# A decoder trunk on one core: row sums ordered behind weight splits, two homes for branch weights, an early weight's split ordered behind the last output weight's

## The chip, the core and the metric

The kernel runs on one core of a Trainium2 chip. A core has five engines that run side by side, each through its own stream of instructions in order: TensorE (PE; matrix products, with PEld its weight loads), VectorE (DVE), ScalarE (ACT), GpSimd (POOL) and SyncE (SP, which here only issues transfers). The metric is the device time of one execution in microseconds (us), as the median of several runs. The profile is of one further execution.

## The reference

One layer of a decoder trunk on x of 512 tokens by 1024 channels, in float32: a conditioned norm, one input projection, two attention branches, two gates, an output projection with residual, then a second conditioned norm and a gated MLP with a short convolution.

```python
mod = cs @ w_ada[l] + b_ada[l]
shift1, scale1, gate1, shift2, scale2, gate2 = [m[:, None, :] for m in jnp.split(mod, 6, axis=-1)]
h = _rmsnorm(x, norm1_g[l]) * (1.0 + scale1) + shift1
proj = h @ w_in[l]
qa, ka, va, qd, kd, vd, ga, gd = jnp.split(proj, points, axis=-1)
...
merged = (jax.nn.sigmoid(ga) * (out_a @ w_branch_swa[l])
          + jax.nn.sigmoid(gd) * (out_d @ w_branch_diff[l]))
x = x + gate1 * (merged @ w_out[l])
h2 = _rmsnorm(x, norm2_g[l]) * (1.0 + scale2) + shift2
x = x + gate2 * _conv_ffn(h2, w_up[l], conv_w[l], conv_b[l], w_down[l])
return _rmsnorm(x, final_g)
```

## The kernel before

Every float32 product is made of three products of split operands: a value is split into a high part (a cast on ScalarE, L102) and a low part (a subtraction on VectorE, L103), and high by high, high by low and low by high are summed (`mm3`, L105). So each weight that arrives from memory passes ScalarE, then VectorE, then TensorE. Such a pass is called a split here. `split_pair` (L95) makes it into two rotating buffers, tags "whi" and "wlo" with three places each; `split` (L101) makes it into a tile that is given.

Raw weights arrive in tiles of 512 KB with the tag "raw", which has four places for all of them (`raw_tile`, L90). A place is free again when its last reader is done, so a weight that waits for its split keeps the next load back.

The stages, in order: the input projection's first part; the sliding-window attention; the differential attention with the "a" gates; from tick 182 the "d" gates and the merge (eight gate units `wgd`, `pgd` of eight steps, and eight branch units `wbd`, `pB` of four steps, interleaved, L860 to L897); the output projection (`wo`, `oc`); the norm; the MLP's up products (`up`, a scheme that multiplies sums and differences of blocks; its first operands are p1, p2 and m5); the down products (`dc`).

Until the merge is done, TensorE's order is written out by hand through `fill` (L459): each call is one tick, which runs one step of the current unit and loads up to two units ahead (`prefetch`, L454). At the ticks in `ADA_AT` (L30) one further row of the modulation weight is loaded and summed on VectorE: `ada_rows` (L706), 32 rows in all, 17 of them at ticks up to 148 and 15 from tick 180 to 250. These sums give gate1, shift2, scale2 and gate2, which are needed when the output weights are scaled (`g1b`) and after the merge (`g2row`, spread over partitions by TensorE transposes and copied by ScalarE).

The other engines' streams are laid down when the program is built, by a planner. It takes instructions in source order, or by priority where one is given, and its own estimate of when each is ready; on the chip each engine then follows its stream. `tc.high_priority` lets instructions go ahead; `tc.issue_after(ins)` puts those of the same engine as `ins` behind `ins` in the stream, at build, without a wait on the chip. In `ada_rows` the sums have high priority and come behind `behind_dve`, in this stage a VectorE instruction of the attention that has long passed.

The branch weight `wbd` holds two units' weights, so four are made, j = 0, 2, 4 and 6. All four are split into one tile, `gpart(3)` (tag "gT3", one place). Later that tile serves `st` (L1051), whose first half `s_t` is filled by two transfers: a plain load by SP, and one that adds a second block to it, issued by POOL (L1002, L1004). Its split is m5, into a tile of the tag "m5w" (L1059), which nothing else uses before.

The output weights are scaled and split by `load_rows` (L930, `wo`, `wo_h`, `wo_l`), eight of them, two or three ahead of TensorE since "whi" and "wlo" have three places. The early weights p1 and p2 (L1055) come after them in the source, in tiles of their own (`early`). p2's low part is ordered behind the last output weight's low part, `wo_low`.

Of the kernel before, what the change touches and what calls it, by code (L numbers as in the profile page):

```python
# [8 lines left out]
F32 = mybir.dt.float32  # L9
F32R = mybir.dt.float32r  # L10
# [4 lines left out]
P = 128  # L15
D = 1024
S = 512
KT = D // P
# [8 lines left out]
WB = 3  # L27
HP = 100000
ST = 6
ADA_AT = set(range(20, 150, 8)) | set(range(180, 300, 5))  # L30
G1_AT = 12
STAT_LAG = 10
# [9 lines left out]
def kernel(  # L42
# [19 lines left out]
    nc = tc.nc  # L62
    xd, wout, wup, wdown = x[0], w_out[0], w_up[0], w_down[0]
    wba, wbd, od = w_branch_swa[0], w_branch_diff[0], out[0]

    def pool(name, bufs=1, space=None, stack=ctx):
        kw = {} if space is None else {"space": space}
        return stack.enter_context(tc.tile_pool(name=name, bufs=bufs, reuse_waits="tile", **kw))
# [12 lines left out]
    def sbank(name, shape=(P, S)):  # L81
        return bank("s", 3, list(shape), name)
# [7 lines left out]
    def raw_tile(shape, name):  # L90
        return wp.tile(shape, F32, tag="raw", bufs=4, name=name)

    lows = [None]

    def split_pair(raw, shape, name):  # L95
        hi = wp.tile(shape, F32R, tag="whi", bufs=WB, name=name + "_h")
        lo = wp.tile(shape, F32R, tag="wlo", bufs=WB, name=name + "_l")
        lows[0] = split(hi, lo, raw)
        return hi, lo

    def split(hi, lo, src):  # L101
        nc.scalar.copy(hi, src)  # L102
        return nc.vector.tensor_sub(lo, src, hi.bitcast(F32))  # L103

    def mm3(o, lh, ll, rh, rl, start, stop):  # L105
        nc.tensor.matmul(o, lh, rh, start=start, stop=False)  # L106
# [337 lines left out]
    def load_tile(n, name):  # L444
        r = raw_tile([P, KT, P], name)
        nc.sync.dma_start(r, w_tiles[n])
        return split_pair(r, [P, KT, P], name)
# [4 lines left out]
    current, tick, behind_dve = [], [0], [None]  # L452
# [6 lines left out]
    def fill(n):  # L459
        for _ in range(n):  # L460
# [19 lines left out]
            tick[0] += 1  # L480
            if tick[0] in ADA_AT:
                next(ada, None)
# [4 lines left out]
    def steps(o, wts, rhs, nk, k0=0, cl=slice(0, P)):  # L487
        wh, wl = wts
        for k in range(nk):
            mm3(o, wh[:, k, cl], wl[:, k, cl], rhs[0][k0 + k], rhs[1][k0 + k], k == 0, k == nk - 1)  # L490
            if k < nk - 1:
                yield
# [7 lines left out]
    def swa_scores(i, n0):  # L500
        if n0 == 0:
# [4 lines left out]
            c.sb = [ap.tile([P, 2, P], F32, tag="st0", bufs=2, name=f"st{i}_0")]  # L506
            c.sb += [ap.tile([P, 2, 256], F32, tag="st", bufs=ST, name=f"st{i}_{n}") for n in range(1, NT)]
            c.pT = []
# [100 lines left out]
    def diff_scores(*ss):  # L609
# [17 lines left out]
        for s, sps, w in ops:  # L627
# [3 lines left out]
            for m in range(2):  # L631
                st = ap.tile([P, w], F32, tag="st", bufs=ST, name=f"sd{h}_{n}_{m}")
                with tc.high_priority(offset=HP):
# [72 lines left out]
    def ada_rows():  # L706
        for idx in range(32):
            r = raw_tile([P, D], f"ra{idx}")
            nc.sync.dma_start(r, w_ada_t[2 * D + idx * P : 2 * D + (idx + 1) * P, :])
            with tc.high_priority(offset=HP // 2), tc.issue_after(behind_dve[0].ins):  # L710
                nc.vector.tensor_tensor_reduce(r, r, csb, 1.0, 0.0, ALU.mult, ALU.add, late_mod[:, idx : idx + 1])  # L711
            yield

# [3 lines left out]
    def add_gate_a(j):  # L717
        def gate(wts):
            o = fbank(f"pga{j}")
            yield from steps(o, wts, hT, KT)  # L720
            with tc.high_priority(offset=HP):
                nc.scalar.activation(ta[:, j], o, AF.Tanh, scale=0.5)

        def load():
            if j % 2 == 0:
                r = raw_tile([P, 4, 2 * P], f"wba{j}")
                for a in range(2):
                    nc.sync.dma_start(
                        r[64 * a : 64 * a + 64],
                        wba[256 * a : 256 * a + 256, j * P : (j + 2) * P].rearrange("(i p) n -> p i n", p=64),  # L730
                    )
                pair_w["a"] = split_pair(r, [P, 4, 2 * P], f"wba{j}")
            return pair_w["a"]

        def branch(wts):
            o = fbank(f"pA{j}")
            rhs = [[outa[b][:, k] for k in range(4)] for b in range(2)]
            yield from steps(o, wts, rhs, 4, cl=slice(j % 2 * P, j % 2 * P + P))
            nc.vector.scalar_tensor_tensor(ta[:, j], ta[:, j], 1.0, o, ALU.add, ALU.mult)

        units.append((lambda: load_tile(TILE_GA + j, f"wga{j}"), gate))
        units.append((load, branch))

    pairs, firsts, scored, probs, aTs = {}, {}, {}, {}, {}
    ada = ada_rows()
    add_q(2)
    add_q(3)
# [80 lines left out]
    bp = pool("mlp")  # L828

    def gpart(i, shape, name, dt=F32):  # L830
        if i < 2:
            return big.tile(shape, dt, tag=("vvh", "vvl")[i], name=name)
        return bp.tile(shape, dt, tag=f"gT{i}", name=name)
# [9 lines left out]
    g1b = gpart(4, [P, D], "g1b")  # L843
# [25 lines left out]
    def add_merge(j):  # L869
        def load():  # L870
            if j % 2 == 0:
                r = raw_tile([P, 4, 2 * P], f"wbd{j}")
                nc.sync.dma_start(r, wbd[:, j * P : (j + 2) * P].rearrange("(i p) n -> p i n", p=P))
                wb = gpart(3, [P, 2, 4, 2 * P], f"wbd{j}", F32R)
                wh, wl = wb[:, 0], wb[:, 1]
                split(wh, wl, r)
                pair_w["d"] = wh, wl
            return pair_w["d"]

        def branch(wts):  # L880
            o = sbank(f"pB{j}")
            rhs = [[vv[b][:, k] for k in range(4)] for b in range(2)]
            yield from steps(o, wts, rhs, 4, cl=slice(j % 2 * P, j % 2 * P + P))
            td = tds[j]
            nc.vector.scalar_tensor_tensor(td, td, 1.0, o, ALU.add, ALU.mult)
            nc.vector.tensor_add(td, td, ta[:, j])
            split(mgh[j], mgl[j], td)

        units.append((load, branch))
# [32 lines left out]
    def eight(name):  # L922
        return [
            [tbank(name + "0"), tbank(name + "1")],
            [fbank(name + "2"), fbank(name + "3")],
            [sbank(name + "4"), sbank(name + "5")],
            [sbank(name + "6"), vbank(name + "7")],
        ]

    def load_rows(src, k, name, gate):  # L930
        r = raw_tile([P, D], name)
        nc.sync.dma_start(r, src[k * P : (k + 1) * P, :])
        nc.vector.tensor_mul(r, r, gate)
        pair = split_pair(r, [P, D], name)
        return pair

    def tok_proj(acc, lh, ll, wts, nk, done, half_done=None):
        def step(k, t, hfs=(0, 1)):
# [24 lines left out]
    bl = big.tile([P, 3, 4, 256], F32R, tag="hlA", name="bl")  # L963
    braw = {}
    oacc = eight("oc")
    wo = [load_rows(wout, k, f"wo{k}", g1b) for k in range(KT)]

    def add_and_stat(acc, dst, x, wpool, name):
        ss = []
# [29 lines left out]
    W, R = {}, {}  # L999

    def load_raw(dst, blocks):
        nc.sync.dma_start(dst, upblock(*blocks[0]))  # L1002
        for blk in blocks[1:]:
            nc.gpsimd.dma_start(dst, upblock(*blk), accum_op=ALU.add)  # L1004
        return dst
# [16 lines left out]
    SRC = dict(p1="a11", m5="s1", m6="s1", p2="a12", m7="s3", p3="s1", p4="a22")  # L1022

    def sum_w(J, name):
        src = R[J, SRC[name]]
        nc.vector.tensor_add(src, src, R[J, "a11" if name == "m6" else "a12"])  # L1026

    def cast_w(J, name):
        W[J, name] = [
            wp.tile([P, 4, 256], F32R, tag=g, bufs=WB, name=f"{name}_{J}_{g}") for g in ("whi", "wlo")  # L1030
        ]
        nc.scalar.copy(W[J, name][0], R[J, SRC[name]])  # L1032

    def low_w(J, name):
        hi, lo = W[J, name]
        nc.vector.tensor_sub(lo, R[J, SRC[name]], hi.bitcast(F32))  # L1036

    def prep(J, name, dst=None):
        if dst is not None:
            W[J, name] = dst  # L1040
            return split(dst[0], dst[1], R[J, SRC[name]])
        if name in ("m6", "p3"):
            sum_w(J, name)
        cast_w(J, name)
        low_w(J, name)
# [5 lines left out]
    st = gpart(3, [P, 2, 4, 256], "s1_t1")  # L1051
    t1n = st[:, 1]
    R[0, "s1"] = load_raw(st[:, 0], [(0, 1, 0), (0, 1, 1)])
    wo_low = lows[0]
    for i, name in enumerate(("p1", "p2")):  # L1055
        with tc.issue_after(wo_low.ins) if i else ExitStack():
            early_low = prep(0, name, (early_w[i][:, 0], early_w[i][:, 1]))
        W[1, name] = early_w[2 + i][:, 0], early_w[2 + i][:, 1]
    m5w = bp.tile([P, 2, 4, 256], F32R, tag="m5w", name="m5w")  # L1059
    prep(0, "m5", (m5w[:, 0], m5w[:, 1]))  # L1060
    with tc.issue_after(early_low.ins):
        sum_w(0, "m6")
# [371 lines left out]
    for x in range(2):  # L1434
        prep(*ahead.pop(0))
# [336 lines left out]
```

## Time and profile before

| | before |
|---|---|
| median of 3 runs | 688.33 us (688.19 to 689.62) |
| the profiled execution | 686.36 us |
| its span, first to last instruction | 684.6 us |
| mean granted TensorE clock | 0.998 |
| busy: TensorE, its weight loads | 673.5 (98%), 589.6 (86%) |
| busy: VectorE, ScalarE, GpSimd | 556.8 (81%), 383.5 (56%), 65.9 (10%) |
| bytes moved | 119.68 MB, mean 175 GB/s |
| chain that ended last, by engine | PE 78%, DMA 9%, DVE 8%, issue 3%, ACT 1% |

A row of the timeline gives the start in us, the duration in us, the engine, the line of the kernel, the operation, output and inputs, how many were merged, and in brackets the engine's idle time before it and what ended it. A row with a count (x32) and three durations gives the shortest, median and longest in ns and the first and last start. In the list of waits the numbers are us in total, times and the longest. A busy TensorE is not one at its peak, since the ends of matmuls are modelled.

### The profile page before, as it was taken

Reading aid. Unit: us, or ns where it says so; the run is one execution under the profiler, and the core shown is the slowest. Engines: PE = TensorE matmul, PEld = TensorE weight load, DVE = VectorE, ACT = ScalarE, POOL = GpSimd, SP = SyncE. Lnnn points to the kernel's source line nnn. Section 1 sums busy time; section 2 is a strip of 40 time slices with the busy share of each in tenths; the row PEclk is TensorE's granted clock in tenths of the full one; section 3 lists DMA queues with packets and bytes.
Section 4 is the critical chain, followed back from the end, with each engine's and each line's share of the span. In section 5 each row is a group of like instructions: output and inputs, shape, how many; then the busy total and the mean of one; then the engine's idle time right before and its main releaser. Section 6 shows DMA issues by size and latency. Waiting matters only on the chain.

```text
span 684.6 us, 10929 instructions
## 1 busy us (share of the span) xinstructions
PE 673.5 (98%) x4117; PEld 589.6 (86%) x4117; DVE 556.8 (81%) x1036; ACT 383.5 (56%) x678; POOL 65.9 (10%) x74
## 2 busy tenths in 40 slices
PE   8999999999999999999999999999999999999995
PEld 7887777778788888788799999999999998888884
DVE  5996867778775677773689998888888999979997
ACT  6676756454554332441588565666555666656665
POOL 2000000000100000000020110111110003540300
PEclk9999999999999999999999999999999999999999
DMA  9952224454363667347672989787866658996903
GB/s 355 417 214 79 94 85 149 145 170 150 97 183 94 200 236 245 119 161 226 197 124 83 215 226 209 177 200 186 204 170 184 152 171 198 199 204 187 165 1 124
DMA packets 71077, 119.68 MB, mean 175 GB/s; under 512 B 3952, under 2 KB 47728, under 8 KB 71024
## 3 DMA queue, kind: packets, MB, share of 16 engines
q1 hardware_dynamic: 52960, 95.04, 41.8%
q0 software_dynamic: 17776, 23.60, 21.1%
q8 instruction: 32, 0.52, 0.3%
q10 hardware_dynamic: 288, 0.34, 0.2%
q14 instruction: 21, 0.17, 0.1%
HBM read 116.87 MB, written 2.10 MB: 174 GB/s over the span
## 4 chain that ended last, share of the span: by engine, by line
PE 78%; DMA 9%; DVE 8%; issue 3%; ACT 1%; DVEq 0%; POOLq 0%; ACTq 0%
PE up L1098 32%; PE dc L1701 11%; DMA ra<-in_w_ada_t_dram 4%; PE av L345 3%; DMA s_t<-in_w_up_dram 2%; PE pga L106 2%; PE aqa L342 2%; PE pga L107 2%; PE pga L108 2%; PE sd L113 1%; PE pk L106 1%; PE pq L106 1%; DVE ra L711 1%; PE pk L108 1%; PE pq L108 1%
## 5 line engine op out<-in xcount | busy, mean ns | idle before, releaser
L1098 PE MATMUL up<-t,m_whi 128*128 128x256 f32 x512 | 93.1, 283 | 0.0
L1098 PEld LDWEIGHTS up<-t,m_whi 128*128 128x128 f32 x512 | 79.9, 192 | 0.0
L1098 PE MATMUL up<-t,m_wlo 128*128 128x256 f32 x256 | 72.4, 283 | 0.0
L1098 PE MATMUL up<-bh,p_whi 128*128 128x256 f32 x232 | 65.7, 283 | 0.0
L1098 PE MATMUL up<-bl,p_whi 128*128 128x256 f32 x232 | 65.7, 283 | 0.0
L1098 PE MATMUL up<-bh,p_wlo 128*128 128x256 f32 x232 | 65.7, 283 | 0.0
L711 DVE CUSTOM_DVE_ANT_0 ra<-ra,csb 128x1024 f32<-128x1024 f32 x32 | 39.0, 1220 | 16.5 <-DMA ra<-in_w_ada_t_dram 16.5
L1098 PEld LDWEIGHTS up<-t,m_wlo 128*128 128x128 f32 x256 | 49.2, 192 | 0.0
L1098 PEld LDWEIGHTS up<-bh,p_whi 128*128 128x128 f32 x232 | 44.5, 192 | 0.0
L1098 PEld LDWEIGHTS up<-bl,p_whi 128*128 128x128 f32 x232 | 44.5, 192 | 0.0
L1098 PEld LDWEIGHTS up<-bh,p_wlo 128*128 128x128 f32 x232 | 44.5, 192 | 0.0
L1004 POOL DMA_DIRECT2D s<-in_w_up_dram x21 | 27.0, 1365 | 158.1 <-DMA s<-in_w_up_dram 128.9
L1032 ACT CAST m_whi<-s 128x1024 fp32r<-128x1024 f32 x31 | 32.5, 1048 | 15.7 <-DVE s L1026 9.1
L1036 DVE TENSOR_TENSOR m_wlo<-s,m_whi 128x1024 fp32r<-128x1024 f32 x31 | 37.7, 1217 | 1.3 <-ACT m_whi L1032 1.3
L1098 PE MATMUL up<-t,p_whi 128*128 128x256 f32 x176 | 32.2, 283 | 0.0
L648 ACT ACTIVATE sd<-sd,dmx 128x128 f32<-128x128 f32 (+3 forms) x32 | 17.8, 557 | 23.9 <-DVE dmx L646 23.2
L1098 PEld LDWEIGHTS up<-t,p_whi 128*128 128x128 f32 x176 | 27.4, 192 | 0.1
L144 POOL TENSOR_TENSOR r<-ms,mhalf 128x4 f32<-128x4 f32 x4 | 5.1, 1276 | 219.1 <-DVE dls L652 149.6
L1032 ACT CAST p_whi<-wa 128x1024 fp32r<-128x1024 f32 x18 | 18.8, 1043 | 12.6 <-PE up L1098 9.0
L1036 DVE TENSOR_TENSOR p_wlo<-wa,p_whi 128x1024 fp32r<-128x1024 f32 x18 | 22.0, 1222 | 4.0 <-ACT p_whi L1032 3.3
L1105 ACT ACTIVATE gT<-a,cols 128x512 f32<-128x512 f32 x22 | 17.6, 813 | 13.3 <-DVE a L1140 13.0
L1098 PE MATMUL up<-t,p_wlo 128*128 128x256 f32 x88 | 24.9, 283 | 0.0
(517 smaller groups left out, 2018.8 us busy)
## 6 DMA issues: line engine op xcount, KB each, us to landing
ra<-in_w_ada_t_dram SPq DMA_DIRECT2D x32, 512.0 KB, 3.4
wa<-in_w_up_dram SPq DMA_DIRECT2D x22, 512.0 KB, 4.4
s<-in_w_up_dram SPq DMA_DIRECT2D x21, 512.0 KB, 4.6
s<-in_w_up_dram POOLq DMA_DIRECT2D x21, 512.0 KB, 6.6
adaw<-in_w_ada_t_dram SPq DMA_DIRECT2D x15, 512.0 KB, 9.6
a<-in_w_up_dram SPq DMA_DIRECT2D x11, 512.0 KB, 4.9
b<-in_w_down_dram SPq DMA_DIRECT2D x10, 512.0 KB, 4.1
w<-in_w_first_dram SPq DMA_DIRECT2D x8, 512.0 KB, 9.9
```

The costliest lines, as they stand in the source:

```text
L106: nc.tensor.matmul(o, lh, rh, start=start, stop=False)
L107: nc.tensor.matmul(o, lh, rl, start=False, stop=False)
L108: nc.tensor.matmul(o, ll, rh, start=False, stop=stop)
L345: nc.tensor.matmul(acc[i], ht[:, t : t + P], wts[k][w][:, S:], start=start, stop=stop)
L648: nc.scalar.activation(pm[m], pm[m], AF.Exp, bias=mx[:, m : m + 1], scale=slope, accum_out=lsum[:, m : m + 1])
L711: nc.vector.tensor_tensor_reduce(r, r, csb, 1.0, 0.0, ALU.mult, ALU.add, late_mod[:, idx : idx + 1])
L1004: nc.gpsimd.dma_start(dst, upblock(*blk), accum_op=ALU.add)
L1032: nc.scalar.copy(W[J, name][0], R[J, SRC[name]])
L1036: nc.vector.tensor_sub(lo, R[J, SRC[name]], hi.bitcast(F32))
L1098: nc.tensor.matmul(o[u], w[:, k, cu], b[:, k], start=name in ("p1", "m5", "p2") and k == 0 and x == 0, stop=k == 3 and x == 2, skip_group_ ...
L1105: nc.scalar.activation(grow(j), av[J][:, u], AF.Identity, bias=cv[:, 66 + j : 67 + j], scale=cv[:, 44 + j : 45 + j])
L1701: nc.tensor.matmul((bank2[u] if o is None else o)[:, sl], a[:, q, cu], b[:, q, sl], start=first_mm and x == 0, stop=last_mm and x == 2, sk ...
```

## The change

Three things. A list `recent` keeps the low parts of the last two weight splits (on VectorE). From tick 180 (`ADA_LATE`) each row sum is ordered behind both of them, where it was ordered behind `behind_dve`, and so are VectorE's instructions for the first output weight. The branch weights j = 2 and 6 go to a tile of the tag "m5w" instead of "gT3", so that two tiles alternate. And `split` returns both its instructions, so that p2's early split is ordered behind the last output weight's cast on ScalarE as well as its subtraction on VectorE. No instruction that computes is added or removed.

```diff
+ADA_LATE = 180
...
-    lows = [None]
+    casts, lows, recent = [None], [None], [None, None]
...
-        lows[0] = split(hi, lo, raw)
+        casts[0], lows[0] = split(hi, lo, raw)
+        recent[:] = recent[1:] + lows
         return hi, lo
 
     def split(hi, lo, src):
-        nc.scalar.copy(hi, src)
-        return nc.vector.tensor_sub(lo, src, hi.bitcast(F32))
+        return nc.scalar.copy(hi, src), nc.vector.tensor_sub(lo, src, hi.bitcast(F32))
...
-            with tc.high_priority(offset=HP // 2), tc.issue_after(behind_dve[0].ins):
+            with ExitStack() as place:
+                place.enter_context(tc.high_priority(offset=HP // 2))
+                for b in recent if tick[0] >= ADA_LATE else behind_dve:
+                    place.enter_context(tc.issue_after(b.ins))
                 nc.vector.tensor_tensor_reduce(r, r, csb, 1.0, 0.0, ALU.mult, ALU.add, late_mod[:, idx : idx + 1])
...
-                wb = gpart(3, [P, 2, 4, 2 * P], f"wbd{j}", F32R)
+                if j % 4:
+                    wb = bp.tile([P, 2, 4, 2 * P], F32R, tag="m5w", name=f"wbd{j}")
+                else:
+                    wb = gpart(3, [P, 2, 4, 2 * P], f"wbd{j}", F32R)
                 wh, wl = wb[:, 0], wb[:, 1]
-                split(wh, wl, r)
+                casts[0], lows[0] = split(wh, wl, r)
+                recent[:] = recent[1:] + lows
...
-    wo = [load_rows(wout, k, f"wo{k}", g1b) for k in range(KT)]
+    with tc.issue_after(recent[0].ins), tc.issue_after(recent[1].ins):
+        wo = [load_rows(wout, 0, "wo0", g1b)]
+    wo += [load_rows(wout, k, f"wo{k}", g1b) for k in range(1, KT)]
...
-    wo_low = lows[0]
+    wo_cast, wo_low = casts[0], lows[0]
     for i, name in enumerate(("p1", "p2")):
-        with tc.issue_after(wo_low.ins) if i else ExitStack():
+        with ExitStack() as behind_wo:
+            if i:
+                behind_wo.enter_context(tc.issue_after(wo_cast.ins))
+                behind_wo.enter_context(tc.issue_after(wo_low.ins))
             early_low = prep(0, name, (early_w[i][:, 0], early_w[i][:, 1]))
```

`prep` takes the second of the two instructions that `split` now returns; `load_rows` returns the pair without naming it first.

More of the change, by code (lines that the diff above doesn't have):

```diff
@@ L933, in load_rows @@
         nc.vector.tensor_mul(r, r, gate)
-        pair = split_pair(r, [P, D], name)
-        return pair
+        return split_pair(r, [P, D], name)
     def tok_proj(acc, lh, ll, wts, nk, done, half_done=None):
@@ L1040, in prep @@
             W[J, name] = dst
-            return split(dst[0], dst[1], R[J, SRC[name]])
+            return split(dst[0], dst[1], R[J, SRC[name]])[1]
         if name in ("m6", "p3"):
```

## The prediction

> **What bounds the kernel now.** I read the page first, then TensorE's waits, then its timeline around each of them.
>
> ```profile
> span 684.6 us, 10929 instructions
> ...
> PE 673.5 (98%) x4117; PEld 589.6 (86%) x4117; DVE 556.8 (81%) x1036; ACT 383.5 (56%) x678; POOL 65.9 (10%) x74
> ...
> L711 DVE CUSTOM_DVE_ANT_0 ra<-ra,csb 128x1024 f32<-128x1024 f32 x32 | 39.0, 1220 | 16.5 <-DMA ra<-in_w_ada_t_dram 16.5
> ...
> s<-in_w_up_dram POOLq DMA_DIRECT2D x21, 512.0 KB, 6.6
> ```
>
> TensorE (PE) is busy for 98% of the span, so an edit that only reorders the other engines is worth what TensorE waits for them. The row sums (L711) hold VectorE (DVE) idle for 16.5 us, but that is idle time of an engine off the path unless it reaches TensorE. The list of TensorE's waits says where it does:
>
> ```profile
> PE ava L222 <- POOL ones L119: 1.1, 1, 1.1
> PE oc L1155 <- DVE wo_l L103: 0.8, 1, 0.8
> ...
> PE pB L108 <- DVE wbd L103: 0.4, 1, 0.4
> ```
>
> The first is at the start of the kernel. The other two are in the stages that the change touches. How long they are is read from the matmuls' starts in the timeline:
>
> ```profile
> 277.87 0.39 PE L106 MATMUL pB<-vvh,wbd 128*128 128x512 f32 x1
> 278.09 0.39 PE L107 MATMUL pB<-vvl,wbd 128*128 128x512 f32 x1
> 278.92 0.50 PE L108 MATMUL pB<-vvh,wbd 128*128 128x512 f32 x1 [0.44 <-DVE wbd L103]
> ...
> 330.79 0.61 PE L1158 MATMUL oc<-wo_h,mg3l 128*128 128x512 f32 x2
> 331.46 0.50 PE L1154 MATMUL oc<-wo_h,mg3h 128*128 128x512 f32 x1
> 332.72 0.50 PE L1155 MATMUL oc<-wo_l,mg3h 128*128 128x512 f32 x1 [0.76 <-DVE wo_l L103]
> ```
>
> Such matmuls start about 0.23 us apart (277.87 to 278.09). The step from 278.09 to 278.92 is 0.83: 0.60 lost. The pair at 330.79 takes 0.67 to the next start instead of 0.45: 0.22 lost. The step to 332.72 is 1.26: 1.03 lost. Stall A (the branch weight) is 0.60, stall B (the last output weight) 1.25, together 1.85 us.
>
> ```profile
> 270.00:280.00 10.00, 9.56 (x43) 7.58 (x42) 8.27 (x14) 3.60 (x5) 0.00 (x0) 1.00 0.65 213
> 290.00:300.00 10.00, 10.00 (x46) 8.29 (x45) 8.47 (x10) 2.94 (x4) 0.00 (x0) 1.00 0.32 105
> 310.00:320.00 10.00, 10.00 (x46) 8.29 (x45) 0.69 (x1) 1.77 (x2) 0.00 (x0) 1.00 0.97 282
> 330.00:340.00 10.00, 9.19 (x40) 7.08 (x39) 8.19 (x14) 5.36 (x10) 0.00 (x0) 1.00 0.64 198
> ```
>
> After the times, the columns are PE, its weight loads, DVE, ACT, POOL, the granted clock (1.00 throughout), the DMA share and GB/s. By busy matmul time the two windows with stalls miss 0.44 and 0.81, together 1.25 us. By weight loads they miss 0.71 and 1.21 of 8.29 in ten, which is 0.86 and 1.46, together 2.3. I keep 1.85, from the starts. The Trainium skill, "Perfetto Trace Analysis", section "Identifying the Most-Contended Engine", says that matmul busy time misjudges the headroom because matmuls are pipelined, and that weight-load busy time is the better measure. By that rule the sum would be 2.3 instead of 1.25; the starts agree with the rule more than with the busy time.
>
> Whether a microsecond saved there reaches the end is in the chain of waits:
>
> ```profile
> 356.06 216.11 PE up L1098 x1800
> 572.17 74.18 PE dc L1701 x327
> ```
>
> From 356 to 646 the end is set by TensorE alone, without a break, so what is gained before it should arrive whole.
>
> **The change part by part.** *Second home for the branch weights.* Four such weights (j = 0, 2, 4, 6) share one tile; now two alternate.
>
> ```profile
> 255.20 0.38 SPq L873 DMA_DIRECT2D wbd<-in_w_branch_diff_dram  x1
> 274.52 1.04 ACT L102 CAST wbd<-wbd 128x1024 fp32r<-128x1024 f32 x1
> 277.65 1.22 DVE L103 TENSOR_TENSOR wbd<-wbd,wbd 128x1024 fp32r<-128x1024 f32 x1
> 289.29 0.39 PE L108 MATMUL pB<-vvh,wbd 128*128 128x512 f32 x1
> L108 PE MATMUL pB<-vvh,wbd x32: 388/389/504, 245.7 to 300.2; 128*128 128x512 f32 x32
> wgd<-in_w_tiles_dram SPq DMA_DIRECT2D x8, 512.0 KB, 4.4
> ```
>
> The third weight (j = 4) was loaded at 255.20 and split only at 274.52 (ScalarE's half) and 277.65 (VectorE's half, until 278.87): that is stall A. A load of this size lands in 4.4, so its data lay idle from about 260, waiting for the previous weight's last matmul. The other tile is free once the second of the eight products (245.7 to 300.2) has ended, an estimated 256. So the split can run at about 260 to 262, sixteen microseconds ahead of use. Stall A goes: -0.60. No matmul, split or load is added. As a by-product the raw buffer (one of four for all these loads) is held some 7 us instead of 24, so later loads start earlier.
>
> *Row sums behind weight splits.* From tick 180 on, 15 of the 32 row sums are ordered on VectorE behind the two latest weight splits, where before they were free to go ahead of them.
>
> ```profile
> 221.93 1.23 DVE L711 CUSTOM_DVE_ANT_0 ra<-ra,csb 128x1024 f32<-128x1024 f32 x1 [4.78 <-DMA ra<-in_w_ada_t_dram]
> 224.92 0.33 SPq L446 DMA_DIRECT2D wgd<-in_w_tiles_dram  x1
> 230.25 1.05 ACT L102 CAST wgd_h<-wgd 128x1024 fp32r<-128x1024 f32 x1 [5.83 <-PE pga L107]
> 247.94 0.39 PE L106 MATMUL pgd<-hThA,wgd_h 128*128 128x512 f32 x1
> ```
>
> The order is laid down at build, nothing waits on the chip for it. What it can cost is a raw buffer held longer. The sum of 221.93 must now follow the split whose cast ends at 231.3. The load of 224.92 used the buffer that this sum freed, so it moves to about 232.6, when that cast and a subtraction of 1.22 are over. It lands at 237, is split by 239.4 (1.05 + 1.22), and its first matmul is at 247.94. It is 8.5 us early, and the cost is nothing. If that cover were gone, the price would be one load and split, 6.7. The bound on the other side is a VectorE wait for a row that moves from ahead of a split to behind it: at most 4.78, also within the cover. I take 0. Fifteen sums are 18.3 us of work (1220 ns each) in the 78 us between 222 and 300, and nothing on TensorE needs them before the last branch product ends, past 300. The first output weight, tied in the same way, is not due before then either.
>
> *The end of the stage.* The early weights' split (L1057) for p2 is now ordered behind the last output weight's on ScalarE (ACT) as well as VectorE, and the home change frees the tile behind s_t earlier.
>
> ```profile
> 300.59 0.38 SPq L1002 DMA_DIRECT2D s_t<-in_w_up_dram  x1
> 305.74 1.49 POOL L1004 DMA_DIRECT2D s_t<-in_w_up_dram  x1 [76.45 <-DMA s_t<-in_w_up_dram]
> 318.23 1.05 ACT L102 CAST m5w<-s_t 128x1024 fp32r<-128x1024 f32 x1 [10.21 <-DMA s_t<-in_w_up_dram]
> 319.18 2.00 ACT L102 CAST wo_h<-wo 128x1024 fp32r<-128x1024 f32 x2
> 327.27 1.05 ACT L102 CAST wo_h<-wo 128x1024 fp32r<-128x1024 f32 x1
> 328.52 0.39 PE L1154 MATMUL oc<-wo_h,mg2h 128*128 128x512 f32 x1
> 329.41 1.05 ACT L102 CAST early<-wa 128x1024 fp32r<-128x1024 f32 x1 [1.09 <-DMA wa<-in_w_up_dram]
> 330.36 1.05 ACT L102 CAST wo_h<-wo 128x1024 fp32r<-128x1024 f32 x1
> 331.44 1.23 DVE L103 TENSOR_TENSOR wo_l<-wo,wo_h 128x1024 fp32r<-128x1024 f32 x1 [1.67 <-ACT wo_h L102]
> ```
>
> Stall B has two causes. One is p2's cast at 329.41, which waits 1.09 for its load and stands ahead of the last output weight's cast (330.36). The tie takes it away. That cast then waits only for its buffer, whose last reader is the matmul before 328.52. It starts at about 328.6, ends at 329.7, the subtraction ends at about 331.0, and TensorE, undelayed, wants the result at about 331.5: 0.5 to spare, -1.25. The second cause is upstream: ACT stood 10.21 us for s_t (the m5 split) with output weights queued behind it. The s_t load waited for the shared tile until 300.4, when the last branch product ended. Now that tile's last reader is the product that ends with the matmul of 289.29, so the load can go at 289.5. It took 5.2 until its accumulating half was issued (300.59 to 305.74): 294.7. This half landed 12.4 later while the DMA share was 0.97; its kind has a median of 6.6, and in 290 to 300 the share is 0.32. So it lands between 301.3 and 307.1, and I take 301.3, by the share. On SP's queue the load goes ahead of what is issued between 290 and 300.6, at 0.38; POOL had nothing else to issue (it waited 76.45). The m5 split cannot come before 300.4 anyway, since its own tile is now the second home.
>
> The sum against the profiled execution: span 684.6 - 0.60 - 1.25 = 682.75. That execution took 686.36, 1.76 around the span, and 684.5 with the gain. The median shown is 688.33, 1.97 above it; I put the difference on the median: 686.5.
>
> **The rivals.** *Only stall A goes.* The spare of 0.5 us in B is thin, and the first early weight (p1) is not tied; if its split falls between the last two output weights, 1.05 on ACT or 1.22 on DVE use it up. Against it: its load, freed of the 10 us standstill, should land long before. Time: 688.33 - 0.60 = 687.7.
>
> *More than the stalls.* With p2 and m5 out of the way, the chain into the next stage (norms and transposes until 356) may lose its own small gaps; less than 1 us is there to be had. About 685.7.
>
> *Slower: the m5 split in front of the gate rows.* This split can now be planned at 300.4 on ACT, ahead of the copies that free two TensorE banks.
>
> ```profile
> 301.46 1.07 ACT L852 COPY g2row<-pg 128x512 f32<-128x512 f32 x2
> 305.40 0.39 PE L1154 MATMUL oc<-wo_h,mg0h 128*128 128x512 f32 x1
> ```
>
> If s_t lands only at 307.1, then 1.05 and 1.07 later (309.2) the banks are free, and TensorE wanted them at 305.40: 3.8 lost, less 1.85 gained, +1.95, or 690.3. It begins to cost when s_t lands after 303.3 and eats the whole gain from 305.1, which is 10.4 after its issue. The 12.4 speaks for it; the median of 6.6 and the lower share speak against. The Trainium skill, "TensorE: Matmul & The Clock Gate", Part 1, says that an idle TensorE longer than about 3.4 us falls to half clock and needs as long to recover. By that rule this case would cost an estimated 1.7 us more, near 692; no run here shows it, as the longest idle time above is 1.1 us at a granted clock of 1.00.
>
> *It does not do what it says:* the planner leaves the order as it was, 688.3.
>
> **How the numbers follow.** The forecast 686.5 has 0.61, only stall A 0.15, more 0.07, slower 0.14, nothing 0.03. No change is within 0.2%, 1.4 us, about what a measurement of this kernel can tell: 686.95 to 689.7. Of the forecast's 0.61, 0.06 falls above 686.95. So faster has 0.55 + 0.07 = 0.62, the same 0.06 + 0.15 + 0.03 = 0.24, slower 0.14. The forecast alone spans 685.9 to 687.2 (stalls by busy time or by weight loads). The range reaches from 685.3 to 689.4: the cases on the fast side and those without effect, with the slower one left out but for its mildest form.
>
> **What would show it.** The branch weights' splits start within about 7 us of their loads and TensorE's wait for wbd is gone. The s_t load is issued near 290, ACT's wait for it shrinks from 10.2 to under 2, and the last output weight's cast precedes p2's. The early-weight matmuls and the long stretch after 356 start 1.9 us earlier, and the tail keeps its length. I am wrong if TensorE shows a new wait at the gate rows near 305, if a weight of pgd arrives late after 230, or if the gain is there at 356 and gone at the end.

## The result, and the profile after

| | before | after |
|---|---|---|
| median, same session | 688.87 us (688.19 to 689.62, 6 runs) | 685.44 us (685.25 to 687.89, 6 runs) |
| ratio, with its 95% interval | | 0.9965 (0.9949 to 0.998) |
| profiled execution | 686.36 | 685.34 |
| its span | 684.6 | 683.6 |

The change is faster by 0.35%. The forecast was 686.5 us, inside a range of 685.3 to 689.4. On the medians the gain is 3.4 us where 1.85 was forecast; between the two profiled executions it is only 1.0. Both differences are explained below.

First the page of the changed kernel: the span, the busy times, and the row sums, whose last column is VectorE's idle time ahead of them.

```profile
span 683.6 us, 10927 instructions
...
PE 671.9 (98%) x4117; PEld 589.1 (86%) x4117; DVE 557.8 (82%) x1036; ACT 383.9 (56%) x678; POOL 65.9 (10%) x74
...
L715 DVE CUSTOM_DVE_ANT_0 ra<-ra,csb 128x1024 f32<-128x1024 f32 x32 | 38.6, 1220 | 0.1
```

The row sums stood 16.5 us for their rows; now it is 0.1. Next, TensorE's waits (total, times, longest):

```profile
PE ava L223 <- POOL ones L120: 1.1, 1, 1.1
PE aka L249 <- DVE cols L253: 1.1, 1, 1.1
PE oc L1166 <- DVE tdall L893: 0.8, 1, 0.8
```

The waits for wbd (stall A) and for the last output weight (stall B) have left the list. The third line is new. In the timeline around it the columns are start, duration, engine, line, operation, and in brackets the idle time before it and its releaser:

```profile
300.77 1.05 ACT L104 CAST m5w<-s_t 128x1024 fp32r<-128x1024 f32 x1 [1.99 <-DMA s_t<-in_w_up_dram]
301.73 1.07 ACT L856 COPY g2row<-pg 128x512 f32<-128x512 f32 x2
301.92 1.23 DVE L941 TENSOR_TENSOR wo<-wo,g1b 128x1024 f32<-128x1024 f32 x1 [2.41 <-DMA wo<-in_w_out_dram]
302.43 0.61 PE L1170 MATMUL oc<-wo_h,mg0l 128*128 128x512 f32 x2
303.07 0.68 DVE L893 SCALAR_TENSOR_TENSOR tdall<-tdall,pB 128x512 f32<-128x512 f32 x1
303.80 0.50 PE L1166 MATMUL oc<-wo_h,mg0h 128*128 128x512 f32 x1 [0.76 <-DVE tdall L893]
```

A pair like the one at 302.43 is followed after 0.45 (two steps of 0.23); here the next matmul starts 1.37 later, so 0.92 us are lost: stall C. TensorE needs the bank that the last merge product (303.07) reads. That product stood on VectorE behind the scaling of the seventh output weight (301.92), which had waited 2.41 for its load. The two gate-row copies, 0.54 each, were done at 302.80, so this time it was VectorE's order and not ScalarE's.

What becomes of the gain further on is in the chain of waits:

```profile
354.39 216.13 PE up L1110 x1800
570.53 74.19 PE dc L1713 x327
```

The long stretch starts 1.67 us earlier than before (356.06) and lasts as long (216.13 and 216.11), so what is gained ahead of it is kept until the down products, and up to the issue of the last output transfer (680.89 before, 679.25 after). From there to the end of the span 3.70 us pass before and 4.33 after, so 1.0 of the 1.64 is left. And not all of the 1.67 comes from the stalls: 1.85 less 0.92 is 0.93. Another 0.39 stands already at the first product of the "d" gates (232.95 and 232.56), which came at 232.30 in a second execution of the kernel before; so that part is scatter. The remaining 0.35 is in steps too small to be counted as stalls.

### The profile page after: what moved, and what is told of

Its sections match the earlier page's. It is cut to its first block, busy times and chain, and to the rows that moved or that the text cites. A ratio compares the mean times of both kernels' runs of the same rounds, so it can differ in the third digit from the quotient of the medians.

```text
span 683.6 us, 10927 instructions
## 1 busy us (share of the span) xinstructions
PE 671.9 (98%) x4117; PEld 589.1 (86%) x4117; DVE 557.8 (82%) x1036; ACT 383.9 (56%) x678; POOL 65.9 (10%) x74
## 4 chain that ended last, share of the span: by engine, by line
PE 92%; DVE 4%; DMA 1%; issue 1%; ACT 1%; DVEq 0%; ACTq 0%
PE up L1110 32%; PE dc L1713 11%; PE av L346 3%; PE pga L107 2%; PE pga L109 2%; PE pga L108 2%; PE pgd L107 2%; PE pgd L108 2%; PE pgd L109 2%; PE oc L1166 2%; PE oc L1167 2%; PE oc L1170 2%; PE aqa L343 2%; PE sd L114 1%; PE pk L107 1%; PE pq L107 1%
```

## The experiments

In all of them "lost" is the time by which steps between matmul starts are too long, summed between 195 and 345 us of the profiled execution, counting steps over 0.21 us too long, as the prediction did for A and B. The diffs are shortened; those of H, T and the sums without their wait go by the kernel before, the others by the whole change. Letters: R is the ties of the row sums and of the first output weight, H the second home, T p2's tie on ScalarE.

**The second home alone (H).**

```diff
-                wb = gpart(3, [P, 2, 4, 2 * P], f"wbd{j}", F32R)
+                if j % 4:
+                    wb = bp.tile([P, 2, 4, 2 * P], F32R, tag="m5w", name=f"wbd{j}")
+                else:
+                    wb = gpart(3, [P, 2, 4, 2 * P], f"wbd{j}", F32R)
```

> Only the second home for the branch weights; row sums, first output weight and p2's split are ordered as before the change. If the home did the work: no TensorE wait for wbd near 278 (0.60 gone), the s_t load issued near 289 as with the whole change, no 10 us standstill of ScalarE near 310, hence no TensorE wait for the last output weight near 331 (1.25 gone) although p2's split may stand ahead of it; the new wait of the changed kernel near 303 (0.92) is there too. The time is that of the whole change, about 0.35% under before. If the row-sum order did the work: VectorE still waits some 16 us for rows, and the time stays within 0.15% of before.

Measured: 686.68 us, ratio 0.9984 (0.9968 to 0.9999), so less than half of the 0.35% expected. A and B are both gone, and C is 2.65. The edit moves more than a tile: the planner lays VectorE's and ScalarE's streams out anew from 244 us on. The second branch weight's low part, for one, comes at 245.85 and ahead of row sums, where before it came at 260.07 and behind them. The timeline of this kernel shows another door to C than the one above:

```profile
303.64 0.61 PE L1169 MATMUL oc<-wo_h,mg0l 128*128 128x512 f32 x2
305.16 1.04 ACT L104 CAST m5w<-s_t 128x1024 fp32r<-128x1024 f32 x1 [6.45 <-DMA s_t<-in_w_up_dram]
306.11 1.07 ACT L856 COPY g2row<-pg 128x512 f32<-128x512 f32 x2
306.74 0.50 PE L1165 MATMUL oc<-wo_h,mg0h 128*128 128x512 f32 x1 [2.49 <-ACT g2row L856]
```

ScalarE takes the m5 split's cast first and stands 6.45 us for s_t; the gate-row copies that free TensorE's banks come behind it. TensorE starts when the first copy is over (306.11 and half of 1.07). This is the prediction's slower rival, in a mild form.

**p2's tie alone (T).**

```diff
         with ExitStack() as behind_wo:
             if i:
+                behind_wo.enter_context(tc.issue_after(wo_cast.ins))
                 behind_wo.enter_context(tc.issue_after(wo_low.ins))
```

> Only p2's early split behind the last output weight on ScalarE too; one home, row sums as before. If the p2 cast ahead of the last output weight makes the wait near 331: the 1.25 there goes to under 0.2, the wait of 0.60 near 278 and ScalarE's 10 us standstill for s_t stay, no wait near 303; the span is 1.2 to 1.4 shorter, about as much as the whole change brought in its trace (1.25 from 143 us to 354 us). If ScalarE's standstill upstream makes it: the wait near 331 stays above 0.8 and the time is that of before.

Measured: 687.1 us, ratio 0.9983 (0.9972 to 0.9994). In its profiled execution B is smaller (0.21 and 0.42 near 324 and 331; under 0.2 was expected), but 0.94 is lost near 344, where TensorE waits for the norm. The norm's first squares stand on ScalarE behind an early weight's cast that waited 3.95 for its load until 336.29. The branch weights cost more than in the first profile of before, 0.61 and 1.32:

```profile
261.38 0.39 PE L108 MATMUL pB<-vvl,wbd 128*128 128x512 f32 x1
262.22 0.50 PE L109 MATMUL pB<-vvh,wbd 128*128 128x512 f32 x1 [0.45 <-DVE wbd L104]
...
278.45 0.39 PE L108 MATMUL pB<-vvl,wbd 128*128 128x512 f32 x1
280.00 0.50 PE L109 MATMUL pB<-vvh,wbd 128*128 128x512 f32 x1 [1.16 <-DVE wbd L104]
...
344.40 0.99 PE L1206 MATMUL th<-ident,xn 128*128 128x128 f32 x7 [0.73 <-DVE xn L1196]
```

The streams of TensorE, VectorE, ScalarE and GpSimd in this execution are those of the kernel before, but for two casts on ScalarE near 329 that changed places. So the stalls at the branch weights are those of the kernel before, in another run.

**The whole change without the second home (R and T).**

```diff
-                if j % 4:
+                if False:
```

> The whole change without the second home: row sums and the first output weight behind the splits, p2 tied. My theory: the row sums now queue behind branch-weight splits that must wait for TensorE to leave the shared tile, so raw buffers are held and the output weights come later; the wait near 278 stays (0.4 to 1.0) and new ones may come at 300 to 320; time within 0.3% of before, not faster than 687.5. If the order of the row sums were worth something by itself: under 687.0.

Measured: 684.25 us, ratio 0.9945 (0.9929 to 0.9961), clearly faster than expected and below the whole change. No stall A, B or C is left. TensorE's complete list of waits:

```profile
PE ava L223 <- POOL ones L120: 1.1, 1, 1.1
PE aka L249 <- DVE cols L253: 0.8, 1, 0.8
PE av L293 <- DVE sq L303: 0.5, 1, 0.5
PE av L346 <- ACT hThA L332: 0.2, 1, 0.2
```

All four are from the start of the kernel. So the ties take A away with one home, and the home is not needed for it.

**The ties alone (R).** The whole change without the second home and without p2's tie on ScalarE:

```diff
-                if j % 4:
+                if False:
...
-                behind_wo.enter_context(tc.issue_after(wo_cast.ins))
```

> The row sums and the first output weight tied behind the weight splits, and nothing else of the change: one home for the branch weights, p2 tied on VectorE alone. Theory now: the ties alone remove stall A, because in the kernel before the branch weight's subtraction waited on VectorE behind row sums and merge products (cast 274.52, subtraction 277.65), not for its tile; with the ties it follows its cast by about 1.3 us. Stall B (1.25 us) stays or shrinks little. Time 685.0 to 686.2, about 685.5, which is the kernel with ties and p2's tie (684.25) and B on top. Rival, the step of the prediction: the second home is what removes A and the ties are worth 0; then the time is that of the kernel before, 687.7, with A of 0.6 and B of 1.25 both there. Second rival: p2's tie is worth nothing, then 684.3 with no stall near 331.

Measured: 685.19 us (684.25 to 685.36), ratio 0.9943 (0.9927 to 0.9958), nothing lost in the profiled execution. VectorE and ScalarE at the place of stall A, in this kernel:

```profile
272.30 1.06 ACT L104 CAST wbd<-wbd 128x1024 fp32r<-128x1024 f32 x1 [2.06 <-PE pB L109]
273.63 1.22 DVE L104 TENSOR_TENSOR wbd<-wbd,wbd 128x1024 fp32r<-128x1024 f32 x1
274.77 1.22 DVE L715 CUSTOM_DVE_ANT_0 ra<-ra,csb 128x1024 f32<-128x1024 f32 x1
...
277.99 0.39 PE L109 MATMUL pB<-vvh,wbd 128*128 128x512 f32 x1
```

The sums come behind the split. The cast starts when the shared tile is free (272.30), the subtraction is over at 274.85, and TensorE wants it at 277.99: 3.1 us to spare with one home. B, which was expected to stay, isn't there in this execution, the fastest of the five.

**Two further parts.** The home and p2's tie without the ties (H and T), and the home and the ties without p2's (H and R):

```diff
-                for b in recent if tick[0] >= ADA_LATE else behind_dve:
+                for b in behind_dve:
...
-    with tc.issue_after(recent[0].ins), tc.issue_after(recent[1].ins):
+    with ExitStack():
```

> The second home and p2's tie, with the row sums and the first output weight placed as before. Theory now: the home makes the s_t load early, which leaves p2's tie nothing to do, and it puts the m5 split (which waits for s_t) ahead of the gate rows' copies on ScalarE and the seventh output weight's scaling ahead of the last merge product on VectorE; so a stall C of 0.9 to 2.7 us near 303 as in the kernel with the home alone, and the time of that one, 686.7 (686.0 to 687.4). Rival: the row sums are worth nothing beside the home, then it is the whole change, 685.4. Rival: p2's tie is worth its 0.6 here too, then 686.1.

```diff
-                behind_wo.enter_context(tc.issue_after(wo_cast.ins))
```

> The second home and the row sums' ties, without p2's tie on ScalarE. Theory now: with s_t early the p2 split's load has landed long before and the tie changes two places of ScalarE's order only, so it is the whole change: 685.4 (684.8 to 686.0), with a stall near 303 of 0.9 us or more and none near 331. Rival: the tie is needed here too, then a wait for the last output weight of 0.6 to 1.25 near 331 comes back and the time is 686.1 to 686.7.

Measured: H and T 686.84 us, ratio 0.9984 (0.9965 to 1.0002), 1.87 lost near 303: 0.35 by the order on VectorE, 1.53 by the one on ScalarE. H and R 684.9 us, ratio 0.9945 (0.993 to 0.996), 0.53 lost at 304 (0.9 or more was expected), none near 331. With s_t early, p2's tie has nothing left to do.

**Closing C's doors.** First the scaling of the seventh output weight is ordered behind the last merge product; then the m5 cast behind the gate-row copies as well.

```diff
-            nc.vector.scalar_tensor_tensor(td, td, 1.0, o, ALU.add, ALU.mult)
+            merged[0] = nc.vector.scalar_tensor_tensor(td, td, 1.0, o, ALU.add, ALU.mult)
...
-    wo += [load_rows(wout, k, f"wo{k}", g1b) for k in range(1, KT)]
+    wo += [load_rows(wout, k, f"wo{k}", g1b) for k in range(1, 6)]
+    with tc.issue_after(merged[0].ins):
+        wo += [load_rows(wout, 6, "wo6", g1b)]
+    wo += [load_rows(wout, 7, "wo7", g1b)]
```

> The whole change, with the scaling of the seventh output weight ordered on VectorE behind the product of the last merge (j = 7). In the changed kernel this scaling stood ahead of the merge product, waited 2.41 for its load, and TensorE waited 0.92 at 302.7 for the bank that the merge frees. Theory: that wait goes and nothing takes its place, so the long stretch of up products starts 0.9 to 1.0 earlier than in the changed kernel and the time is 0.13% under it (ratio to before about 0.995). Rival: the wait near 303 has another cause (the m5 split, or the gate-row copies), and the time is that of the changed kernel.

Measured: 684.98 us (684.22 to 689.01, four of twelve runs above 688), ratio 0.9973 (0.9955 to 0.9992); what the four lost is in no profile. The gain of 0.13% over the whole change (0.9965) didn't come. The profiled execution has a stall of 1.27 that waits for the other door:

```profile
303.32 0.61 PE L1175 MATMUL oc<-wo_h,mg0l 128*128 128x512 f32 x2
303.46 1.05 ACT L104 CAST m5w<-s_t 128x1024 fp32r<-128x1024 f32 x1 [5.15 <-DMA s_t<-in_w_up_dram]
304.42 1.07 ACT L856 COPY g2row<-pg 128x512 f32<-128x512 f32 x2
305.05 0.51 PE L1171 MATMUL oc<-wo_h,mg0h 128*128 128x512 f32 x1 [1.11 <-ACT g2row L856]
```

```diff
-        nc.scalar.copy(dst[:, hf * S : (hf + 1) * S], pr)
+        last_copy[0] = nc.scalar.copy(dst[:, hf * S : (hf + 1) * S], pr)
...
     spread_rows(g2row, g2c, "pg2")
+    gate_copy = last_copy[0]
...
-    prep(0, "m5", (m5w[:, 0], m5w[:, 1]))
+    with tc.issue_after(gate_copy.ins):
+        prep(0, "m5", (m5w[:, 0], m5w[:, 1]))
```

> The whole change, with the m5 split's cast ordered behind the two copies of the gate rows on ScalarE and the seventh output weight's scaling ordered behind the last merge product on VectorE. Theory now: these two are the only doors of stall C, so no TensorE gap above 0.3 us is left between 195 and 340 and the profiled span is about 682.6; median 684.0 to 684.8, about 684.4, as the kernel without the second home (684.25). Rival: the early s_t load costs elsewhere, since what waits for it now holds VectorE and ScalarE later (m5's subtraction stands ahead of the last product's low half): a gap of 1 us or more behind 305, median 685.2 or above. If the home gives something of its own beside the ties, the median is below 684.0.

Measured: 684.17 us (683.98 to 684.7), ratio 0.9934 (0.9919 to 0.9949), nothing lost:

```profile
301.62 1.23 DVE L946 TENSOR_TENSOR wo<-wo,g1b 128x1024 f32<-128x1024 f32 x1 [1.52 <-DMA wo<-in_w_out_dram]
302.40 0.62 PE L1179 MATMUL oc<-wo_h,mg0l 128*128 128x512 f32 x2
302.86 0.39 PE L1175 MATMUL oc<-wo_h,mg0h 128*128 128x512 f32 x1
```

The weight's load is as late as in the changed kernel (301.62 and 301.92), but TensorE goes on after 0.46. With both orders C is gone. The time is then that of the kernel without the second home (684.25), so no gain of the home beside the ties is seen.

**The home's price, side by side.** The whole change and the one without the second home once more, on the same chip.

> The whole change once more, beside the one without the second home. Theory now: stall C near 303 (0.5 to 2.7 us, by when s_t lands) is the price of the home, so 685.0 to 686.0, and slower than the one without the home by 0.6 to 1.3. Rival: the home costs nothing and the two agree within 0.4.

> The whole change without the second home, once more, on the chip of the whole change. Theory now: 683.9 to 684.6, below the whole change in every round but one at most. Rival: the first time was lucky, and the median is 685 or more.

Measured: the whole change 685.65 us (685.19 to 686.68), ratio 0.9963 (0.9949 to 0.9977); without the home 684.22 us (683.92 to 684.62), ratio 0.9941 (0.9927 to 0.9955). The runs do not overlap; the home costs 1.4 us, a little more than the 0.6 to 1.3 expected. The profiled execution of the whole change loses 2.12 at C this time, by ScalarE's door.

**A second look at the kernel before.** No edit.

> The kernel before, profiled once more. The first profiled execution took 686.36 us against medians of 687.7 to 688.9, so it was one of the quicker ones. Theory now: the rest is no constant but stalls that vary from run to run, where a row sum that waits for its row holds VectorE and the weight splits behind it. Then an execution near the median (687.5 to 689) shows TensorE waits for weight splits of 3 to 5 us in all between 195 and 345 us, at other places than the first one or longer ones, beside 14 us or more of VectorE's idle time ahead of the row sums. Rival, as the prediction had it: the rest lies evenly on every stage or around the span, and such an execution has the same two stalls of 0.6 and 1.25. If it is a quick one again (below 686.8), it tells nothing.

Measured: 688.34 us. VectorE and TensorE at the place of stall A:

```profile
275.06 1.04 ACT L102 CAST wbd<-wbd 128x1024 fp32r<-128x1024 f32 x1
276.72 1.23 DVE L933 TENSOR_TENSOR wo<-wo,g1b 128x1024 f32<-128x1024 f32 x1 [0.80 <-DMA wo<-in_w_out_dram]
277.82 0.39 PE L107 MATMUL pB<-vvl,wbd 128*128 128x512 f32 x1
277.87 0.68 DVE L885 SCALAR_TENSOR_TENSOR tdall<-tdall,pB 128x512 f32<-128x512 f32 x1
278.46 1.22 DVE L103 TENSOR_TENSOR wbd<-wbd,wbd 128x1024 fp32r<-128x1024 f32 x1
279.74 0.50 PE L108 MATMUL pB<-vvh,wbd 128*128 128x512 f32 x1 [1.53 <-DVE wbd L103]
```

The cast is over at 276.1, and the subtraction could follow; but VectorE's stream has the first output weight's scaling and a merge product ahead of it, and the scaling has waited for its load. Here A is 1.69, with 0.25 at 261 (a row sum that waited 1.79 for its row stands ahead there), 0.55 at 324, and 0.40 and 1.03 at 333: 3.93 in all, against 1.85 in the quicker execution. VectorE stood 17.4 us for the rows. So the theory's size holds; but at the largest stall it is a weight's scaling that waits, not a row sum.

**The sums without their wait.** The late sums read a row that is at hand.

```diff
...
+            late = idx >= 17
+            if late:
+                nc.gpsimd.tensor_copy(touch[:, idx : idx + 1], r[:, 0:1])
+            dst, row = (junk, csb) if late else (r, r)
-            with tc.high_priority(offset=HP // 2), tc.issue_after(behind_dve[0].ins):
-                nc.vector.tensor_tensor_reduce(r, r, csb, 1.0, 0.0, ALU.mult, ALU.add, late_mod[:, idx : idx + 1])
+            with tc.high_priority(offset=HP // 2), tc.issue_after((recent[0] if late else behind_dve[0]).ins):
+                nc.vector.tensor_tensor_reduce(dst, row, csb, 1.0, 0.0, ALU.mult, ALU.add, late_mod[:, idx : idx + 1])
```

> The kernel before, whose 15 late row sums read the conditioning row, which is at hand, in place of the loaded row, so the numbers of three gates are not the reference's; each row is still loaded, and one of its columns is read by GpSimd, which frees its buffer. The late sums are ordered behind the second latest weight split, about where they stood. So VectorE has the same work among the weight splits and no wait for a row. Theory now: the wait is what costs, not the 1.22 us of a sum ahead of a split. Then no TensorE wait for a branch weight above 0.3 is left and the time is 684.0 to 685.5, with little spread. Rival: the sums' own time ahead of the splits is what costs, then stall A or its like stays and the time is 686.5 or more, spread over 3 us as before.

Measured: 688.54 us (685.1 to 691.16), ratio 0.9998 (0.998 to 1.0017). The theory missed the time. The profiled execution was the quickest of the runs (685.10), so it doesn't show what the usual ones lose; it has no stall at the branch weights, and one of 1.01 of the same kind elsewhere:

```profile
213.28 1.22 DVE L718 CUSTOM_DVE_ANT_0 junk<-csb 128x1024 bf16<-128x1024 f32 x1
...
215.66 0.39 PE L107 MATMUL od<-aTh,vvh 128*128 128x512 f32 x1
216.16 0.68 DVE L408 TENSOR_TENSOR aTl<-td,aTh 128x512 fp32r<-128x512 f32 x1
216.90 0.50 PE L108 MATMUL od<-aTl,vvh 128*128 128x512 f32 x1 [0.85 <-DVE aTl L408]
```

A sum of 1.22 stands three places ahead of the low part that TensorE waits for. But this place is the edit's own doing: in the kernel before, that sum came behind the low part (215.93 and 215.33). The sums are not about where they stood, as the expectation had it. With no row to wait for, the planner placed them anew; the last three run from 277.96 to 281.99, where before the last one started at 270.72. So the run doesn't separate the wait from the place of the sums, and it also frees the raw buffers earlier. What the slower of these runs lose is open.

**All profiled executions together.** "Rest" is the execution's time less what it lost.

| kernel | time | lost | rest |
|---|---|---|---|
| before, first and second | 686.36, 688.34 | 1.85, 3.93 | 684.51, 684.41 |
| T | 687.91 | 3.50 | 684.41 |
| H | 686.59 | 2.65 | 683.94 |
| H and T | 686.11 | 1.87 | 684.24 |
| sums without wait | 685.10 | 1.01 | 684.09 |
| whole change, first and second | 685.34, 686.68 | 0.92, 2.12 | 684.42, 684.56 |
| whole change, seventh scaling later | 685.19 | 1.27 | 683.92 |
| H and R | 685.14 | 0.53 | 684.61 |
| R | 684.25 | 0 | 684.25 |
| R and T, first and second | 684.25, 683.92 | 0, 0 | 684.25, 683.92 |
| whole change, both doors closed | 684.11 | 0 | 684.11 |

The rest is 683.9 to 684.6 in all fourteen, while the times run from 683.92 to 688.34. So TensorE's stalls between 195 and 345 us account for the difference between these profiled executions to within 0.7 us, also for that between two executions of one kernel. A difference as small as H and R's 0.53 is within this scatter.

## Why the prediction was right, and where it was not

**Faster, inside the range: right.** Both stalls of the forecast went, and the long stretch starts 1.67 earlier, against 1.9 forecast. That this is so close is luck in part: with C the stalls give only 0.93, and 0.39 was there already at 232.56, as scatter. The stretch after 356 kept its length as said; the tail didn't: 0.6 more passes behind the issue of the last transfer. Two of the signs that were named, in the changed kernel:

```profile
256.40 0.38 SPq L877 DMA_DIRECT2D wbd<-in_w_branch_diff_dram  x1
262.07 1.05 ACT L104 CAST wbd<-wbd 128x1024 fp32r<-128x1024 f32 x1 [1.72 <-DMA wbd<-in_w_branch_diff_dram]
...
328.68 1.05 ACT L104 CAST wo_h<-wo 128x1024 fp32r<-128x1024 f32 x1 [4.43 <-PE oc L1170]
329.64 1.04 ACT L104 CAST early<-wa 128x1024 fp32r<-128x1024 f32 x1
```

The third branch weight is split 5.7 us after its load, 16 us ahead of use, and the last output weight's cast stands ahead of p2's.

**What takes A away: half right.** The step gave it to the second home, and the home alone does it. But the ties were put at 0, neither gain nor loss, and they are the best part: R alone has 0.9943, the whole change 0.9963 and 0.9965. The step looked for what the ties delay and found it covered, which was right in its numbers (the wgd load at 232.20, forecast 232.6). It didn't ask what the ties, which cover the first output weight too, let pass ahead. It also read the shared tile as the cause of the late split. The first profile shows what came last:

```profile
272.20 0.39 PE L108 MATMUL pB<-vvh,wbd 128*128 128x512 f32 x1
273.08 1.05 ACT L102 CAST wgd_h<-wgd 128x1024 fp32r<-128x1024 f32 x1 [1.62 <-DMA wgd<-in_w_tiles_dram]
275.91 1.23 DVE L933 TENSOR_TENSOR wo<-wo,g1b 128x1024 f32<-128x1024 f32 x1 [0.52 <-DMA wo<-in_w_out_dram]
```

The tile was free when the matmul of 272.20 had ended. The cast came only at 274.52, since ScalarE first did a gate weight's cast that had waited 1.62 for its load. The subtraction at 277.65 stood behind the first output weight's scaling, which had waited 0.52 for its load, and a merge product. So the tile was not what came last. Whether the row sums' ties or the first output weight's do more was not tried apart; in the profiles without the ties a scaling stands ahead of the stall at 278 and a row sum ahead of the small one at 261.

**What takes B away: right, with one reason too many.** p2's tie alone leaves 0.63 in the one look, where the two executions of before have 1.25 and 1.98; but that look loses 0.94 at the norm instead, so the profile doesn't show where the 0.6 us that the tie alone gains on the medians come from. The early s_t load takes all of B, and with R it is gone from the profiled execution without either. R alone has a median of 685.19 and R with T 684.25 and 684.22, so the tie may be worth up to 0.9 there; the quick execution that was profiled doesn't show where.

**s_t early: right, and the slower rival came with it.** The forecast load at 289.5, accumulating half at 294.7 and landing at 301.3 were 289.04, 294.33 and 300.77 in the first profile. But 301.3 was the early end: in the other kernels with the home and the m5 cast first, the cast started at 303.4 to 305.2, and C grew with it (the first two differ by when TensorE arrived, and 0.35 of the 1.87 is VectorE's):

| m5 cast starts | 303.44 | 303.46 | 304.77 | 304.91 | 305.16 |
|---|---|---|---|---|---|
| lost at C | 0.53 | 1.27 | 1.87 | 2.12 | 2.65 |

The choice of 301.3 rested on the DMA share of 0.32 in 290 to 300. With the load moved there, the row of the changed kernel reads:

```profile
290.00:300.00 10.00, 10.00 (x49) 8.35 (x48) 5.22 (x6) 2.79 (x4) 1.49 (x1) 1.00 0.63 154
300.00:310.00 10.00, 9.24 (x42) 7.32 (x41) 5.48 (x6) 5.06 (x7) 0.00 (x0) 1.00 0.48 165
```

The share there is 0.63, since the change moves its own loads into the gap (the next output weight at 288.66 and 296.11, s_t between them). The rival's mechanism was right and its size too small: by its sum a landing at 304.9 or 305.2 costs 1.6 or 1.9, and 2.1 and 2.65 came. It took TensorE to want the bank at 305.40, as in the stalled kernel; in the five executions of the table TensorE wants it at 303.8 to 304.8. It also counted both gate-row copies (1.07), while TensorE goes on after the first, 1.58 behind the start of the cast. So it begins to cost from about 302.2 to 303.3, and not only from 303.3. The prediction named a new wait at the gate rows near 305 as a sign of being wrong: the first execution of the whole change doesn't have it, the second does (2.12). Its 0.14 was too little, and it came as a part of the result rather than as another result. The second row is C itself: 0.76 by matmul busy time, 1.03 by the weight loads (8.35 less 7.32), 0.92 by the starts. The Trainium skill, "Perfetto Trace Analysis", section "Identifying the Most-Contended Engine", prefers the weight loads to matmul busy time for TensorE; here the starts lie between the two.

**The size: the term that was mis-sized is the sum itself.** It was 1.85, from one execution, and the 1.97 between it and the median was put on both sides as if it were constant. The second look shows that it is not: that execution, 688.34, loses 3.93. A median run of before (688.5) is 4.2 above the 684.3 that is left without stalls. So by this estimate the change removes some 4.2, not 1.85, and gives back 0.9 to 2.1 at C; 2.1 to 3.3 are left, and the medians show 3.4 and 2.9. The forecast came out near because an undersized gain and an omitted loss partly cancelled. The measured 685.44 lies closest to the rival "more than the stalls" (685.7), but by the table the gain is in the stalls and not in the chain behind them.

## What to carry to other kernels

When an engine's stream is laid down at build, ask of each instruction that waits for a load not only whether it is late itself, but what stands behind it: a scaling or a split of a later weight, or a row sum, turns the scatter of transfers into stalls of the engine that sets the end. Before taking a stall's size from one profile, compare its time with the median; if the execution was quicker, part of the stalls is not in it. And when an edit makes a transfer start earlier, check what may now be planned behind its arrival: here both gate-row copies came behind a cast that nobody needed yet, and ordering two instructions gave back 1.3 to 1.5 us (685.44 and 685.65 against 684.17, which were not run side by side).

## What was not expected of the hardware

An idle TensorE of 2.65 us kept its clock. The windows around stall C in the kernel with the home alone (after the window, its length, PE, weight loads, DVE, ACT, POOL, the granted clock, the DMA share, GB/s):

```profile
304.00:308.00 4.00, 1.51 (x7) 0.97 (x6) 1.76 (x2) 2.02 (x3) 0.00 (x0) 1.00 0.03 5
308.00:312.00 4.00, 4.00 (x19) 3.30 (x18) 1.55 (x3) 3.05 (x4) 0.00 (x0) 1.00 0.73 235
```

The granted clock is 1.00 in both, so this stall cost no clock. And the spread between runs differs with the order of the streams: R and T took 683.8 to 685.72 us in twelve runs, the kernel before 686.16 to 690.47 in those beside them.
